# An mLSTM and HGRN2 decoder layer on one core: order of clearing, weight splits and the first head's convolution

## The chip, the core and the metric

The kernel runs on one core of a Trainium2 chip. The core has a matrix engine (TensorE, PE below; its weight loads are listed as PEld), and three engines that work on elements: VectorE (DVE), ScalarE (ACT) and GpSimd (POOL). SyncE (SP) issues the DMA transfers. Each engine runs its own instructions in order and waits for semaphores. PE writes to banks of PSUM; DVE and ACT read them from there, which is called an evacuation below. The metric is device time in microseconds, the median of several executions; lower is better.

## What is computed

One inference step of one layer, for 1024 prompt tokens and 8 sequences of 8 tokens (1088 tokens in all), in float32. The input is normalised and multiplied with one large matrix; its columns feed an mLSTM group of 4 heads and an HGRN2 group of 8 heads, whose results are multiplied with an output matrix. Cut to what the change touches:

```python
xn = rmsnorm(x, g_norm)
proj = xn @ w_in                     # 1024 x 7168
xm, zm, om, fh, qh, ih, zh = split(proj)
xc, conv_new = causal_conv(xm, conv_buf, conv_w, conv_b)   # 4 taps
xc = silu(xc)
q, k = per head: xc_h @ w_q, xc_h @ w_k
v = per head: xm_h @ w_v
gates = concat([q, k, v]) @ w_gate + b_gate
ig, lf = gates[..., :4], log_sigmoid(gates[..., 4:])
# mLSTM: running maximum m_t = max(logD over s <= t, cumsum(lf) + m0), then
#   decayed products of q, k and v by chunks
# HGRN2: S_t = diag(f_t) S_{t-1} + k_t v_t^T, o_t = S_t^T q_t, by levels of halving blocks
y = x + concat([hm, oh]) @ w_out
```

## The kernel before

**Split operands.** A float32 product is made from three matmuls of rounded operands: every operand is split into a high part (a cast on ACT) and a low part (a subtraction on DVE or POOL). Lines 94, 95 and 96 are the three matmuls. The normalised input lies in XH and XL.

**Blocks.** `w_in` is worked in blocks of 128 columns. `blk_load` loads a block's raw weights (wraw, three buffers, shared with the weights of q, k and v), `blk_split` splits them (line 147: whi on ACT, wlo on DVE for blocks in `v_splits`, else on POOL; two buffers each). `in_block` (line 246) multiplies a block with the tokens in three pieces of 384, 384 and 320 columns, each in one PSUM bank of a pool of three (`ps_mm`), and calls an evacuation for each piece. When it starts on a block it loads the block after next and splits the next one.

**The front.** Blocks 0 to 7 are xm, two for each of the 4 mLSTM heads. Blocks 0 and 1 run together while the input is still being normalised and transposed, then comes `front_v(0)` (v and the gates of head 0: nine tiles of 128 tokens, six matmuls each), block 2 (`third`), `front_qk(0)` (q and k: eight tiles of 272 columns, six matmuls each), block 3 (`fourth`). Head h of the next three then has `front_v(h)`, block 2h+2, `front_qk(h)` and block 2h+3.

- The evacuation of a piece of xm (`evac` in `front_conv`) makes mh (L477, ACT), a copy XB for the convolution (L478, ACT) and ml (L479, DVE); the last piece has copies for the 64 sample tokens besides (L481 and L482 on ACT, L483 on DVE). The bank is free when all of them have read it.
- `convolve` is a generator with one step at a time: four operations over 1112 columns on DVE (L503 once, L506 three times), a sigmoid on ACT (L514, L515), a product on DVE (L517, L518), the write of xc to memory, the split of xc (xch, L520 on ACT; xcl, L522, on DVE for the first head and on POOL for the others).
- `front_v` copies every tile out with two ACT copies, L540 (values) and L541 (gates, into GTOK for head 0 and GST for the others).

Up to block 3 the order on PE, ACT, DVE and POOL is that in which the code is written (`manual_schedule` in the main part, which calls `next` on the convolutions `c0`, `c1` of head 0 at hand-picked points). After it a scheduler orders all engines but keeps each engine's order fixed in the compiled program; behind the gates PE's order is by hand again. `behind(i, r)` adds an order on instruction i to come after r.

**The gates' scan.** `gate_scan` writes the gates to memory, reads them back as rows of tokens (lf, t1, ig, y), clears one column in t1 (L604), and runs two scans on DVE. It runs beside the first HGRN2 head (`hgrn_main(0)`), whose first level needs the products Q (L1022, L1023) and K (L987) from ACT and DVE; PE's first level is a burst of small matmuls at L101. `ctxs["k2"]` is set to a copy on DVE right behind K's.

Of the kernel before, what the change touches and what calls it, by code (L numbers as in the profile page):

```python
# [17 lines left out]
T = 1088  # L18
TP = 1024
# [11 lines left out]
def hybrid_step(  # L31
# [8 lines left out]
    V, S, G, PE = nc.vector, nc.scalar, nc.gpsimd, nc.tensor  # L40
# [78 lines left out]
    r = 0  # L119
# [22 lines left out]
    def w_split(key, eng=G):  # L142
        raw = wq[key]
        hi = wp.tile([P, 1024], F32R, tag="whi", name=nm("whi"))
        lo = wp.tile([P, 1024], F32R, tag="wlo", name=nm("wlo"))
        wq[key] = (hi.rearrange("p (k c) -> p k c", c=P), lo.rearrange("p (k c) -> p k c", c=P))
        return S.copy(hi, raw), eng.tensor_tensor(lo, raw, f32(hi), op=ALU.subtract)  # L147
# [16 lines left out]
    def blk_load(i):  # L164
        if i < len(blocks) and ("w", i) not in wq:
            kind, j = blocks[i]
            o = boff[kind] + j * P
            return w_load(("w", i), w_in[0, :, o:o + P].rearrange("(k p) c -> p k c", p=P))

    def blk_split(i, eng=None):  # L170
        if i < len(blocks) and not isinstance(wq[("w", i)], tuple):
            return w_split(("w", i), eng or (V if i in v_splits else G))
# [78 lines left out]
    def in_block(*items):  # L251


        ws = []
        for kind, j, evac in items:
            i = bidx[(kind, j)]
            if i > 1 or len(items) == 1:
                if ("w", i) in wq and not isinstance(wq[("w", i)], tuple):
                    blk_split(i)
            ws.append(i)  # L260
        for i in ws:
            blk_load(i + 2)
        nxt = ws[-1] + 1
        if len(items) == 1:
            blk_split(nxt)
        for c, (t0, n) in enumerate(CH):
            xh, xl = xchunk(XH, c), xchunk(XL, c)
            for (kind, j, evac), i in zip(items, ws):
                wh, wl = wq[("w", i)]
                ps = ps_mm()  # L270
                for k in range(8):
                    mm3(ps[:, :n], (wh[:, k, :], wl[:, k, :]), (xh[:, k, :], xl[:, k, :]), k == 0, k == 7)
                    if k % 2 and k < 7:
                        yield cost(6, n)
                evac(c, t0, n, ps)
                yield cost(6, n)
# [8 lines left out]
    ctxs = {}  # L285
# [93 lines left out]
    def behind(i, r):  # L379

        if r is None:
            return
        tc.add_manual_dep(getattr(i, "ins", i), getattr(r, "ins", r).name, mybir.DependencyInfo(
            mybir.DependencyClass.NoSync, mybir.DependencyReason.DATA), reason="behind")
# [42 lines left out]
    GTOK = cp.tile([P, 9, 8], F32, name="GTOK")  # L427
    GST = cp.tile([P, 9, 8], F32, name="GST")
# [96 lines left out]
    def front_v(h):  # L525
        wh, wl = qkv_w[h]
        xms = [fr[2 * h + a]["m"] for a in range(2)]
        for t in range(9):
            ps = ps_mm()
            u = t % 2  # L530
            if u == 0:
                vt = half("vt")
                vv = vt[:, :2 * VW].rearrange("p (a c) -> p a c", c=VW)
                G.memset(vv[:, :, 256:257], 1.0)
                G.memset(vv[:, :, 257:258], 0.0)
            for a in range(2):
                o = 512 + a * 264
                mm3(ps[:, :264], (xms[a][0][:, t * P:(t + 1) * P], xms[a][1][:, t * P:(t + 1) * P]),
                    (wh[:, o:o + 264], wl[:, o:o + 264]), a == 0, a == 1)
            S.copy(vv[:, u, 0:256], ps[:, :256])  # L540
            S.copy((GST if h else GTOK)[:, t, :], ps[:, 256:264])  # L541
            if t == 8:
                nc.sync.dma_start(out=vsd[h], in_=vt[:, :VW])
            elif u:
                nc.sync.dma_start(out=vd[h, :, (t - 1) * VW:(t + 1) * VW], in_=vt[:, :2 * VW])
            yield

        if h:
            V.tensor_tensor(GTOK, GTOK, GST, op=ALU.add)
# [33 lines left out]
    def gate_scan():  # L583

        ig, y, lf, t1, m, b = [unit(s)[0:4, :T] for s in ("ig", "gy", "glf", "gt", "gm", "gb")]

        lg = half("lg")
        LF = lg[:, 0:272]
        V.tensor_scalar(GT, GT, scalar1=bgt, scalar2=None, op0=ALU.add)
        S.activation(LF, GT, AF.Abs)  # L590
        S.activation(LF, LF, AF.Exp, scale=-1.0)
        S.activation(LF, LF, AF.Ln, bias=1.0)
        V.scalar_tensor_tensor(LF, GT, 0.0, LF, op0=ALU.min, op1=ALU.subtract)
        for i, src in enumerate((GT, LF)):
            nc.sync.dma_start(out=gd[i], in_=src)
        for i, dst in ((1, lf), (1, t1), (0, ig), (0, y)):
            nc.sync.dma_start(out=dst.rearrange("p (j t) -> p j t", t=272),
                              in_=gd[i].rearrange("(j r) t -> r j t", r=32)[4 * i:4 * i + 4])
        yield 1.0
        lfs = lf[:, TP:T].rearrange("p (b c) -> p b c", c=8)[:, :, 0]  # L600
        igs = ig[:, TP:T].rearrange("p (b c) -> p b c", c=8)[:, :, 0]
        lm = small(8, "lm")
        behind(V.tensor_tensor(lm[0:4, :], lfs, m0t, op=ALU.add), ctxs["k2"])
        V.memset(t1[:, TP:T].rearrange("p (b c) -> p b c", c=8)[:, :, 0], -1e30)  # L604
        V.tensor_tensor(y[:, TP:T].rearrange("p (b c) -> p b c", c=8)[:, :, 0], igs, lm[0:4, :], op=ALU.max)
        V.tensor_tensor_scan(m, t1, y, initial=0.0, op0=ALU.add, op1=ALU.max)
        yield 4.0
        G.memset(t1, 1.0)
        G.memset(t1[:, 0:TP].rearrange("p (b c) -> p b c", c=P)[:, :, 0], 0.0)
        G.memset(t1[:, TP:T].rearrange("p (b c) -> p b c", c=8)[:, :, 0], 0.0)  # L610
        st = lf[:, 0:TP].rearrange("p (b c) -> p b c", c=P)[:, 1:8, 0]
        V.tensor_tensor(st, st, m[:, 0:TP].rearrange("p (b c) -> p b c", c=P)[:, 0:7, 127], op=ALU.add)
        V.tensor_copy(lfs, lm[0:4, :])
        V.tensor_tensor_scan(b, t1, lf, initial=0.0, op0=ALU.mult, op1=ALU.add)
        V.tensor_tensor(y, b, m, op=ALU.subtract)
        nc.sync.dma_start(out=rd, in_=y)
        V.tensor_tensor(ig, ig, b, op=ALU.subtract)
        nc.sync.dma_start(out=o_pm[0, 0].unsqueeze(1), in_=m[:, TP - 1:TP])
        msl = small(8, "msl")
        V.tensor_copy(msl[0:4, :], m[:, TP:T].rearrange("p (b c) -> p b c", c=8)[:, :, 7])  # L620
        nc.sync.dma_start(out=o_sm[0].rearrange("b h -> h b"), in_=msl[0:4, :])
        yield 6.5
        ps = ps_o()
        for t in range(8):
            PE.transpose(ps[:, t * 8:t * 8 + 4], ig[:, t * P:t * P + P], ident[0:4, 0:4])
            PE.transpose(ps[:, t * 8 + 4:t * 8 + 8], m[:, t * P:t * P + P], ident[0:4, 0:4])
        for j in range(4):
            for o, src in ((64, ig), (68, m)):
                PE.matmul(ps[32 * j:32 * j + 32, o:o + 4], lhsT=src[:, TP + win(j):TP + win(j) + 32],
                          rhs=ident[0:4, 0:4], start=True, stop=True)  # L630
        V.tensor_copy(COLS.rearrange("p a b -> p (a b)"), ps[:, :72])
        S.activation(COLS[:, :, 4:8], COLS[:, :, 4:8], AF.Exp, scale=-2.0)
        yield 0.5

        co = unit("co")
        for kk in range(2):
            pt = ps_o()
            for k in range(4):
                PE.transpose(pt[:27, k * P:(k + 1) * P], CS[:, kk * 4 + k, :], ident)
            V.tensor_copy(co[:27, kk * 512:(kk + 1) * 512], pt[:27, :])  # L640
        nc.sync.dma_start(out=o_pconv[0, 0], in_=co[0:3, :DM])
        nc.sync.dma_start(out=o_sconv[0].rearrange("b j d -> (b j) d"), in_=co[3:27, :DM])
        yield 0.5
# [765 lines left out]
    def run(gen):  # L1409
        for _ in gen:  # L1410
            pass
# [56 lines left out]
    with tc.manual_schedule(engines={ET.PE, ET.Activation, ET.DVE, ET.Pool}):  # L1468
# [63 lines left out]
        blk_split(2, V)  # L1532
        run(prep)
        c0, c1 = convs
        next(c0)
        run(islice(first, 4))
        run(first)
        next(c0)
        next(c1)
        run(front_v(0))  # L1540
        next(c0)
        convs = []
        third = front_conv(1, (2,), convs)
        prep = qkv_prep(1)
        next(prep)
        run(islice(third, 2))
        next(c0)
        next(c1)
        run(islice(third, 2))
        next(c1)  # L1550
        run(c0)
        next(c1)
        run(islice(third, 4))
        run(c1)
        next(prep)
        run(islice(third, 4))
        run(third)
# [164 lines left out]
```

## Time and profile before

| | before |
|---|---|
| median of 3 runs | 1149.5 us (1148.18 to 1153.0) |
| profiled execution, its own time | 1149.5 us |
| its span, first to last instruction | 1147.7 us |
| mean granted TensorE clock | 0.995 |
| ACT busy | 471.1 us (41%) |
| POOL busy | 239.7 us (21%) |
| moved by DMA | 133.53 MB, mean 116 GB/s |

A row of the timeline has the start, the duration, the engine, the line, the operation, output and inputs by the program's names without their numbers, shape, and how many instructions were merged; in brackets stands how long the engine was idle before it, and what ended that. A row of the view of waits has engine, tile and line that waited, what it waited for, total, times and longest. A row of the view by windows has the stretch, its length, busy time of PE, PEld, DVE, ACT and POOL, the granted clock (1.00 is full), the DMA engines' share and GB/s.

### The profile page before, as it was taken

What the parts mean: (1) busy time and instruction counts of PE and PEld (TensorE: products, weight loads), DVE (VectorE), ACT (ScalarE), POOL (GpSimd) and SP (SyncE); (2) the same over time, 40 slices, a digit from 0 to 9 for tenths busy, and PEclk for the clock granted to TensorE, in tenths of its full rate; (3) what the DMA queues carried; (4) which work ended last, traced back from release to release, by engine and by line L of the source; (5) the groups of instructions that cost most, each with busy time, mean ns of one, the idle gap of its engine ahead of it and who ended that gap; (6) DMA issues with size and microseconds to landing.
All of it is one profiled execution on the core that took longest, in us unless ns stands there. A gap on an engine that the chain in (4) does not pass through costs nothing.

```text
span 1147.7 us, 22956 instructions
## 1 busy us (share of the span) xinstructions
PE 1123.9 (98%) x9255; PEld 1056.0 (92%) x9255; DVE 749.7 (65%) x1484; ACT 471.1 (41%) x1047; POOL 239.7 (21%) x396
## 2 busy tenths in 40 slices
PE   7989999899999999999999999999999999999997
PEld 6889999899999999999999999999999998888886
DVE  6656454494778567784779567877677687545533
ACT  6455455335432553235423453252524344243332
POOL 3204333002530144203530153102020200100000
PEclk9999999999999999999999999999999999999999
DMA  7243342222324242334124331422221255567662
GB/s 225 85 150 123 113 157 101 86 56 94 104 83 152 60 152 78 119 95 136 56 78 153 117 112 60 134 77 78 57 78 57 68 171 159 153 196 208 191 191 91
DMA packets 154154, 133.53 MB, mean 116 GB/s; under 512 B 11500, under 2 KB 130376, under 8 KB 154048
## 3 DMA queue, kind: packets, MB, share of 16 engines
q1 hardware_dynamic: 154046, 132.06, 36.9%
q8 instruction: 73, 1.20, 0.4%
q14 instruction: 33, 0.27, 0.1%
q10 hardware_dynamic: 2, 0.00, 0.0%
HBM read 93.47 MB, written 38.57 MB: 115 GB/s over the span
## 4 chain that ended last, share of the span: by engine, by line
PE 88%; DVE 5%; ACT 3%; DMA 2%; issue 2%; POOL 0%; SPq 0%; POOLq 0%; DVEq 0%; ACTq 0%
PE mm L94 24%; PE mm L95 23%; PE mm L96 23%; PE lv L101 2%; PE o L1216 1%; PE o L1235 1%; PE o L94 1%; PE o L95 1%; PE o L96 1%; PE o L1238 1%; DMA mraw<-mixd 1%; PE lv L1197 1%; PE o L1130 1%; PE mm L1338 1%; PE mm L1340 1%
## 5 line engine op out<-in xcount | busy, mean ns | idle before, releaser
L94 PE MATMUL mm<-XH,whi 128*128 128x384 f32 (+1 forms) x1344 | 450.4, 335 | 0.0
L95 PE MATMUL mm<-XL,whi 128*128 128x384 f32 (+1 forms) x1344 | 439.4, 327 | 0.4 <-DVE XL L245 0.4
L96 PE MATMUL mm<-XH,wlo 128*128 128x384 f32 (+1 forms) x1344 | 439.2, 327 | 0.0
L94 PEld LDWEIGHTS mm<-XH,whi 128*128 128x128 f32 x1344 | 253.5, 189 | 3.1 <-issue 2.5
L95 PEld LDWEIGHTS mm<-XL,whi 128*128 128x128 f32 x1344 | 253.5, 189 | 1.8 <-issue 0.9
L96 PEld LDWEIGHTS mm<-XH,wlo 128*128 128x128 f32 x1344 | 252.9, 188 | 0.0
L147 ACT CAST whi<-wraw 128x1024 fp32r<-128x1024 f32 x54 | 56.7, 1051 | 87.2 <-PE mm L95 67.2
L147 POOL TENSOR_TENSOR wlo<-wraw,whi 128x1024 fp32r<-128x1024 f32 x30 | 71.8, 2392 | 84.3 <-ACT whi L147 84.0
L1328 ACT CAST mhi<-mraw 128x1024 fp32r<-128x1024 f32 (+1 forms) x32 | 31.9, 998 | 69.3 <-PE mm L95 50.5
L974 POOL MEMSET A<- 128x288 f32 x8 | 2.7, 342 | 261.8 <-ACT A L1103 261.8
L94 PE MATMUL mm<-XH,mhi 128*128 128x512 f32 x144 | 56.8, 395 | 0.0
L96 PE MATMUL mm<-XH,mlo 128*128 128x512 f32 x144 | 56.3, 391 | 0.2 <-DVE mlo L1329 0.2
L95 PE MATMUL mm<-XL,mhi 128*128 128x512 f32 x144 | 56.1, 389 | 0.0
L1329 DVE TENSOR_TENSOR mlo<-mraw,mhi 128x1024 fp32r<-128x1024 f32 (+1 forms) x32 | 37.0, 1155 | 20.2 <-ACT mhi L1328 19.7
L922 DVE TENSOR_SCALAR f<-f,OML,LB 128x384 f32<-128x384 f32 (+1 forms) x24 | 32.9, 1369 | 10.7 <-ACT f L920 10.3
L479 DVE TENSOR_TENSOR xml<-mm,xmh 128x384 fp32r<-128x384 f32 (+1 forms) x24 | 12.3, 511 | 42.2 <-ACT XB L478 42.2
L96 PE MATMUL mm<-woh,mlo 128*128 128x512 f32 x96 | 37.5, 390 | 0.0
L147 DVE TENSOR_TENSOR wlo<-wraw,whi 128x1024 fp32r<-128x1024 f32 x24 | 29.3, 1220 | 12.5 <-ACT whi L147 12.5
L94 PE MATMUL mm<-woh,mhi 128*128 128x512 f32 x96 | 37.4, 389 | 0.0
L95 PE MATMUL mm<-wol,mhi 128*128 128x512 f32 x96 | 37.4, 389 | 0.0
L990 DVE TENSOR_TENSOR QK<-hk,Sf 128x256 f32<-128x256 f32 x96 | 36.1, 416 | 0.0
L1401 POOL TENSOR_TENSOR rs<-rs,mhalf 128x1 f32<-128x1 f32 (+1 forms) x9 | 4.9, 542 | 145.9 <-DVE rs L1400 145.9
(365 smaller groups left out, 2201.0 us busy)
## 6 DMA issues: line engine op xcount, KB each, us to landing
wraw<-in_w_in SPq DMA_DIRECT2D x56, 512.0 KB
woraw<-in_w_out SPq DMA_DIRECT2D x16, 512.0 KB
mraw<-mixd SPq DMA_DIRECT2D x16, 512.0 KB
mraw<-mixd SPq DMA_DIRECT2D x16, 448.0 KB
xcd<-XB SPq DMA_DIRECT2D x8, 544.0 KB
qkd<-qk SPq DMA_DIRECT2D x16, 272.0 KB
xcr<-xcd SPq DMA_DIRECT2D x8, 544.0 KB
mixd<-xcr SPq DMA_DIRECT2D x8, 544.0 KB
```

Source lines behind the costliest of these rows:

```text
L94: PE.matmul(out, lhsT=lh, rhs=rh, start=first, stop=False)
L95: PE.matmul(out, lhsT=lh, rhs=rl, start=False, stop=False)
L96: PE.matmul(out, lhsT=ll, rhs=rh, start=False, stop=last)
L101: i = PE.matmul(out, lhsT=lhsT, rhs=rhs, start=start, stop=stop)
L147: return S.copy(hi, raw), eng.tensor_tensor(lo, raw, f32(hi), op=ALU.subtract)
L479: evs.append(V.tensor_tensor(ml[:, t0:t0 + m], ps[:, :m], f32(mh[:, t0:t0 + m]), op=ALU.subtract))
L922: V.tensor_scalar(f[:, s], f[:, s], scalar1=OML[:, h:h + 1], scalar2=LB[:, h:h + 1], op0=ALU.mult, op1=ALU.add)
L990: i = V.tensor_tensor(dst, ksrc, ssrc, op=ALU.mult)
L1130: PE.transpose(pt[:, u * P:(u + 1) * P], iT[:, t * P:(t + 1) * P], ident)
L1197: PE.transpose(tp[:, u * P:(u + 1) * P], sq[:, u * P:(u + 1) * P], ident)
L1328: S.copy(hi[:, :w * n], raw[:, :w * n])
L1329: V.tensor_tensor(lo[:, :w * n], raw[:, :w * n], f32(hi[:, :w * n]), op=ALU.subtract)
```

## The change

Three things are put elsewhere in the order; no operation is added or removed.

1. In `gate_scan` the clearing of one column of t1 comes behind `ctxs["k2"]`.
2. `in_block` no longer splits block 3 when block 2 starts; the main part does so, on DVE, behind the first head's convolutions. For later blocks, where a `front_v` ran ahead, the cast of the next block's weights comes behind the gates' copy of v's second tile.
3. The steps of the first head's convolutions: those that stood ahead of the second block's last evacuation come behind it, all steps over the 1112 columns follow each other, and the remaining steps of both come in one run within block 2.

```diff
@@ in_block
-        if len(items) == 1:
-            blk_split(nxt)
+        if len(items) == 1 and nxt > 3:
+            r = blk_split(nxt)
+            if "v1" in ctxs:
+                behind(r[0], ctxs.pop("v1"))
@@ front_v
-            S.copy((GST if h else GTOK)[:, t, :], ps[:, 256:264])
+            gc = S.copy((GST if h else GTOK)[:, t, :], ps[:, 256:264])
+            if t == 1:
+                ctxs["v1"] = gc
@@ gate_scan
-        V.memset(t1[:, TP:T].rearrange("p (b c) -> p b c", c=8)[:, :, 0], -1e30)
+        behind(V.memset(t1[:, TP:T].rearrange("p (b c) -> p b c", c=8)[:, :, 0], -1e30), ctxs["k2"])
@@ the main part
         c0, c1 = convs
-        next(c0)
         run(islice(first, 4))
         run(first)
         next(c0)
+        next(c0)
+        next(c1)
         next(c1)
         run(front_v(0))
         next(c0)
+        next(c1)
+        next(c0)
+        next(c1)
         convs = []
         third = front_conv(1, (2,), convs)
         prep = qkv_prep(1)
         next(prep)
         run(islice(third, 2))
-        next(c0)
-        next(c1)
+        run(c0)
         run(islice(third, 2))
-        next(c1)
-        run(c0)
-        next(c1)
+        run(c1)
+        blk_split(3, V)
         run(islice(third, 4))
-        run(c1)
         next(prep)
```

In the rows below names have the program's numbers; lines of the changed kernel are 2 to 5 higher than before.

DVE at the end of the second block, before: XB_250 and XB_254 are the two convolutions' inputs, Y their sums, mm_564 the bank of the second block's last piece, wraw_260 the raw weights of block 3, mm_722 the third block's first piece.

```order
L503 TENSOR_SCALAR Y_561<-XB_250,PAR 128x1112
L506 SCALAR_TENSOR_TENSOR Y_561<-XB_250,PAR,Y_561 128x1112
L479 TENSOR_TENSOR xml_257<-mm_564,xmh_256 128x256
L483 TENSOR_TENSOR xml_257<-mm_564,xmh_256 128x128
L506 SCALAR_TENSOR_TENSOR Y_561<-XB_250,PAR,Y_561 128x1112 x2
L503 TENSOR_SCALAR Y_600<-XB_254,PAR 128x1112
L506 SCALAR_TENSOR_TENSOR Y_600<-XB_254,PAR,Y_600 128x1112
L147 TENSOR_TENSOR wlo_719<-wraw_260,whi_718 128x1024
L517 TENSOR_TENSOR XB_250<-Y_561,XB_250 128x1024
L518 TENSOR_TENSOR XB_250<-Y_561,XB_250 128x64
L506 SCALAR_TENSOR_TENSOR Y_600<-XB_254,PAR,Y_600 128x1112 x2
L479 TENSOR_TENSOR xml_715<-mm_722,xmh_714 128x384
```

The same place of the changed kernel, from the second half of the evacuation on (mm_559 is the second block's last piece, its first half stands just ahead); mm_732 is the third block's first piece.

```order
L485 TENSOR_TENSOR xml_257<-mm_559,xmh_256 128x128
L505 TENSOR_SCALAR Y_593<-XB_250,PAR 128x1112
L508 SCALAR_TENSOR_TENSOR Y_593<-XB_250,PAR,Y_593 128x1112 x3
L505 TENSOR_SCALAR Y_600<-XB_254,PAR 128x1112
L508 SCALAR_TENSOR_TENSOR Y_600<-XB_254,PAR,Y_600 128x1112 x3
L519 TENSOR_TENSOR XB_250<-Y_593,XB_250 128x1024
L520 TENSOR_TENSOR XB_250<-Y_593,XB_250 128x64
L519 TENSOR_TENSOR XB_254<-Y_600,XB_254 128x1024
L520 TENSOR_TENSOR XB_254<-Y_600,XB_254 128x64
L524 TENSOR_TENSOR xcl_707<-XB_250,xch_706 128x1088
L481 TENSOR_TENSOR xml_729<-mm_732,xmh_728 128x384
L524 TENSOR_TENSOR xcl_711<-XB_254,xch_710 128x1088
```

Both convolutions now run through behind the evacuation, and the split of block 3 has gone behind the second xcl: it is the row after the last one shown, followed by the evacuation of the third block's second piece.

ACT at the start of `front_v(1)`, before: mm_1012 is the last piece of block 3, mm_1066, mm_1078 and mm_1088 are v's first three tiles, wraw_937 the raw weights of block 5.

```order
L147 CAST whi_1184<-wraw_937 128x1024
L477 CAST xmh_935<-mm_1012 128x256
L478 COPY XB_933<-mm_1012 128x256
L540 COPY vt_1067<-mm_1066 128x256
L541 COPY GST<-mm_1066 128x8
L540 COPY vt_1067<-mm_1078 128x256
L541 COPY GST<-mm_1078 128x8
L481 COPY XB_933<-mm_1012 128x8x8
L482 CAST xmh_935<-mm_1012 128x128
L540 COPY vt_1089<-mm_1088 128x256
```

And in the changed kernel:

```order
L479 CAST xmh_935<-mm_1012 128x256
L480 COPY XB_933<-mm_1012 128x256
L542 COPY vt_1067<-mm_1066 128x256
L543 COPY GST<-mm_1066 128x8
L483 COPY XB_933<-mm_1012 128x8x8
L484 CAST xmh_935<-mm_1012 128x128
L542 COPY vt_1067<-mm_1078 128x256
L543 COPY GST<-mm_1078 128x8
L147 CAST whi_1184<-wraw_937 128x1024
L542 COPY vt_1089<-mm_1088 128x256
```

The cast of block 5 has moved from ahead of the evacuation to behind the second tile's copies, and the last evacuation's second half (L483, L484) ahead of the second tile's; heads 2 and 3 have the same. On POOL the subtraction of the same split moves behind two small copies (L500, L501). On SP the load that waits for that split moves behind two more writes of v.

DVE at the first level, before: hq is the HGRN2 query, wlo_2378 the low part of a later block's weights, Q_319 and K_320 are what the level multiplies, glf and gt are the gates' rows lf and t1.

```order
L604 MEMSET gt_2342 4x8
L147 TENSOR_TENSOR wlo_2378<-wraw_2252,whi_2377 128x1024
L930 TENSOR_TENSOR hq_2062<-hq_2062,mm_2312 128x320
L1023 TENSOR_TENSOR Q_319_2364<-hq_2062,f_2060 128x544
L987 COPY K_320_2367<-hk_2061 128x256
L987 COPY K_320_2367<-hk_2061 128x4x64
L1038 COPY Sf_2363<-f_2060 128x544
L603 TENSOR_TENSOR lm_2459<-glf_2341,m0t 4x8
```

And in the changed kernel:

```order
L147 TENSOR_TENSOR wlo_2378<-wraw_2252,whi_2377 128x1024
L934 TENSOR_TENSOR hq_2062<-hq_2062,mm_2312 128x320
L1027 TENSOR_TENSOR Q_319_2364<-hq_2062,f_2060 128x544
L991 COPY K_320_2367<-hk_2061 128x256
L991 COPY K_320_2367<-hk_2061 128x4x64
L1042 COPY Sf_2363<-f_2060 128x544
L607 TENSOR_TENSOR lm_2459<-glf_2341,m0t 4x8
L608 MEMSET gt_2342 4x8
```

The clearing has moved behind K's copies and Sf's, and behind the sum that already waited for them.

## Prediction

> **What bounds the kernel now.** Line numbers are those of the kernel before; times are µs from the start of the span. The page first:
>
> ```profile
> span 1147.7 us, 22956 instructions
> PE 1123.9 (98%) x9255; PEld 1056.0 (92%) x9255; DVE 749.7 (65%) x1484; ACT 471.1 (41%) x1047; POOL 239.7 (21%) x396
> ```
>
> TensorE (PE) is busy 98% of the span. The change adds no arithmetic and, by the compiled order, leaves PE's own order as it was. So it can only act on the moments in which PE stands still, or runs slowly. The view of waits, for PE alone, names them (total, times, longest); three of its rows lie where the diff lies:
>
> ```profile
> PE lv L101 <- DVE K L987: 2.9, 1, 2.9
> PE mm L95 <- DVE xcl L522: 2.2, 1, 2.2
> PE mm L94 <- ACT GST L541: 1.3, 3, 0.4
> ```
>
> I then read the timeline, engine by engine, around each. The profiled execution took 1149.5, its span plus 1.8, and that is also the median of the three runs, so a saving in this trace is subtracted from 1149.5 as it stands.
>
> **Term A: the bank of the second block's last piece.**
>
> ```profile
> 54.16 0.39 PE L94 MATMUL mm<-wqh,xmh 128*128 128x264 f32 x1 [1.61 <-ACT GTOK L541]
> ...
> 51.01 0.38 ACT L478 COPY XB<-mm 128x256 f32<-128x256 f32 x1
> ...
> 51.64 1.38 DVE L506 SCALAR_TENSOR_TENSOR Y<-XB,PAR,Y 128x1112 f32<-128x1112 f32 x1
> 52.94 0.41 DVE L479 TENSOR_TENSOR xml<-mm,xmh 128x256 fp32r<-128x256 f32 x1
> 53.80 0.29 DVE L483 TENSOR_TENSOR xml<-mm,xmh 128x128 fp32r<-128x128 f32 x1 [0.45 <-ACT xmh L482]
> ```
>
> ACT's copy ends at 51.39, but DVE takes a convolution step first and begins the evacuation L479 at 52.94; ACT's last copies wait behind L479, v's copies behind those, and PE's third v tile until 54.16. With the convolution behind the evacuation, L479 starts at 51.42 and the pair L479 to L483 takes 54.09 − 52.94 = 1.15, so the bank is free at 52.58 and PE starts at 52.65. **A = 1.5.** Best and worst: 1.6, the whole wait, and 0.
>
> **Term B: the first q and k tiles.**
>
> ```profile
> 71.58 0.38 PE L94 MATMUL mm<-xch,wqh 128*128 128x272 f32 x1
> ...
> 75.37 0.60 PE L95 MATMUL mm<-xcl,wqh 128*128 128x272 f32 x1 [2.15 <-DVE xcl L522]
> ...
> 79.01 0.29 PE L94 MATMUL mm<-xch,wqh 128*128 128x272 f32 x1
> ...
> 82.87 1.20 PE L101 MATMUL o<-qk,front 128*32 128x272 f32 x16
> ```
> ```profile
> 54.16:56.00 1.84, 1.84 (x15) 1.84 (x16) 1.80 (x2) 0.81 (x5) 1.28 (x3) 1.00 0.38 140
> 75.40:78.60 3.20, 3.02 (x12) 2.73 (x13) 2.34 (x5) 1.08 (x4) 0.28 (x3) 0.50 0.21 64
> ```
>
> Eight tiles of six matmuls run from 71.58 to 82.87: 11.29. The last five, from 79.01, take 3.86, so 0.77 each, and eight at that pace would take 6.2. The other 5.1 are waits and, by the second row of the second fence (granted clock, third number from the end), 3.2 µs at half clock right behind the longest of them. When are the operands there in the changed order?
>
> ```profile
> 54.00 2.78 DVE L506 SCALAR_TENSOR_TENSOR Y<-XB,PAR,Y 128x1112 f32<-128x1112 f32 x2
> 56.70 0.86 DVE L503 TENSOR_SCALAR Y<-XB,PAR 128x1112 f32<-128x1112 f32 x1
> ...
> 63.51 1.23 DVE L147 TENSOR_TENSOR wlo<-wraw,whi 128x1024 fp32r<-128x1024 f32 x1 [4.54 <-ACT whi L147]
> 64.65 1.22 DVE L517 TENSOR_TENSOR XB<-Y,XB 128x1024 f32<-128x1024 f32 x1
> ...
> 65.92 2.78 DVE L506 SCALAR_TENSOR_TENSOR Y<-XB,PAR,Y 128x1112 f32<-128x1112 f32 x2
> ...
> 68.62 0.55 DVE L479 TENSOR_TENSOR xml<-mm,xmh 128x384 fp32r<-128x384 f32 x1
> ...
> 74.03 1.28 DVE L522 TENSOR_TENSOR xcl<-XB,xch 128x1088 fp32r<-128x1088 f32 x1
> ...
> 77.30 0.29 DVE L483 TENSOR_TENSOR xml<-mm,xmh 128x128 fp32r<-128x128 f32 x1 [0.45 <-ACT xmh L482]
> ```
> ```profile
> 66.03 1.10 ACT L520 CAST xch<-XB 128x1088 fp32r<-128x1088 f32 x1 [2.56 <-DVE XB L518]
> ...
> 67.41 0.49 ACT L478 COPY XB<-mm 128x384 f32<-128x384 f32 x1
> ```
>
> From 52.5 DVE runs both convolutions through: each one L503 (0.88 to the next start) and three L506 (2.70 for two, so 1.35 each), 4.93; two end at 62.4. The 4.5 that DVE sat idle before 63.51, held by the split of block 3 that itself waited behind v's copies on ACT, go. Two products L517 with L518 (64.65 to 65.92: 1.27 each) end at 64.95. ACT casts the second xch to 66.1 and takes the third block's first piece to 66.9 (both ACT rows together: 1.87 from 66.03); DVE answers with xml (0.55) and then the second xcl (1.28): ready at 68.7. PE, 1.5 earlier by A, asks for it from 70.1 on: 1.4 of cover, and the waits of B are gone.
>
> **What is late next:** the third tile needs the bank of the third block's last piece, which L483 frees. Before, that came 77.59 − 74.03 = 3.56 after the second xcl began. Now the split of block 3 (1.14 to the next start) and one more xml (0.55) stand between: 67.4 + 3.56 + 1.69 = 72.6. PE has done two tiles at 70.07 + 1.55 = 71.6, so it waits **a new 1.1** until 72.7; six tiles (4.63) later the gate part starts at 77.3 instead of 82.9. Less A, **B = 4.0**. With no new wait it would be 5.1. With one of 2.15 it would be 3.0, and with the half clock back, which costs half of 3.2, 1.4. The first row of the second fence, behind A's wait of 1.6, has full clock, so I take full clock.
>
> The Trainium skill, "TensorE: Matmul & The Clock Gate", Part 1, has the clock halved after an idle window of about 3.4 µs, on windows that run freely. By it neither wait here (2.15, and 2.93 in D) would have to cost any clock, and the gain would be 3.0 less (a rival below); the row shows the half clock behind a wait of 2.15, so the sum goes by the row.
>
> Block 3's split itself is used only by the fourth block, behind the gate part. On SP the load of block 5's raw weights now waits for it, behind two xc writes; block 5's cast stands at 97.31 in a row of C, over 20 µs of cover. POOL's small history copies only change places.
>
> **Term C: three heads' v tiles.** One head stands for three (the wait row says three times 0.4):
>
> ```profile
> 97.25 0.28 PE L94 MATMUL mm<-wqh,xmh 128*128 128x264 f32 x1
> ...
> 103.97 0.28 PE L94 MATMUL mm<-wqh,xmh 128*128 128x264 f32 x1
> ...
> 104.70 0.34 PE L94 MATMUL mm<-XH,whi 128*128 128x384 f32 x1
> ```
> ```profile
> 97.31 1.05 ACT L147 CAST whi<-wraw 128x1024 fp32r<-128x1024 f32 x1 [0.97 <-PE mm L95]
> ...
> 100.36 0.37 ACT L540 COPY vt<-mm 128x256 f32<-128x256 f32 x1 [0.49 <-ACT xmh L482]
> ```
> ```profile
> 98.43 2.39 POOL L147 TENSOR_TENSOR wlo<-wraw,whi 128x1024 fp32r<-128x1024 f32 x1
> ```
> ```profile
> 99.81 1.61 DVE L503 TENSOR_SCALAR Y<-XB,PAR 128x1112 f32<-128x1112 f32 x1 [0.46 <-ACT XB L481]
> ```
>
> Nine tiles take 7.45; the last alone takes 0.73, nine of them 6.57. So 0.88 is lost, not only the 0.4 that the wait names. The cast of the next block stands on ACT ahead of the last evacuation and of v's first copies. Moved behind the second tile's copies, it lets them start 0.9 earlier, and the third tile finds its bank. The fifth tile now takes the bank that L483 frees: L503 starts about 98.9, takes 0.86 (row 56.70) instead of 1.61, because POOL's subtraction no longer runs until 100.82, and L483 ends near 100.0; PE asks at 97.25 + 4 × 0.73 = 100.2. The cast sits between 99.3 and 100.4; the third tile's two copies end by 101.0 at most, and the sixth tile asks at 100.9. Margins of 0.1 to 0.2, so I take the full 0.88: **C = 2.6** for three. Queued behind the cast are seven tiles' copies; if each tile waited out the whole cast, C would be 2.6 − 3 × 1.05 = −0.5.
>
> **Term D: the clearing ahead of the first level.**
>
> ```profile
> 222.25 0.07 DVE L604 MEMSET gt<- 4x8 f32 x1 [5.05 <-DMA gt<-gd]
> 222.33 1.22 DVE L147 TENSOR_TENSOR wlo<-wraw,whi 128x1024 fp32r<-128x1024 f32 x1
> ```
> ```profile
> 218.03 1.05 ACT L147 CAST whi<-wraw 128x1024 fp32r<-128x1024 f32 x1 [1.43 <-PE mm L95]
> ```
> ```profile
> 225.26 0.90 PE L101 MATMUL lv<-Q,K 128*32 128x64 f32 x32 [2.93 <-DVE K L987]
> ...
> 229.04 0.33 PE L95 MATMUL mm<-XL,whi 128*128 128x384 f32 x1
> ```
> ```profile
> 356.62 0.65 PE L101 MATMUL lv<-Q,K 128*32 128x64 f32 x32
> ...
> 358.96 0.33 PE L95 MATMUL mm<-XL,whi 128*128 128x384 f32 x1
> ```
>
> A clearing of 4 by 8 elements holds DVE's queue 5.05 until a transfer lands. PE starts the first level 2.93 after the split at 222.33. Without the clearing the split runs when its cast ends, 219.1, and the level is ready at 222.05; PE is free at 222.33. So the wait of 2.93 goes. From there to the eighth matmul behind the level took 3.78, the same stretch in the next such stage 2.34: 1.44 of slow clock go too. **D = 4.4.** The clearing now stands where DVE arrives at about 222.2, as the transfer lands, so it waits for little; behind it are scans that PE reads much later. Lower end 0, if the copies into K are held by the same transfer.
>
> **Sum:** 1.5 + 4.0 + 2.6 + 4.4 = 12.5; 1149.5 − 12.5 = **1137.0**, 1.1% less.
>
> **Rivals.**
> - *The new wait in B grows past 2 µs and brings the half clock back.* For it: the chain to 72.5 has no gap on DVE. Against: it needs another 1.05. Then B = 1.4: **1139.6**. Chance 0.14.
> - *D does not come*, the change not doing there what it says. For it: K's copies wait on a transfer too. Against: nothing shows one of theirs in flight at 221. **1141.4**. Chance 0.08.
> - *The slow clock is not tied to these waits* (the page's window). The waits go but the slow rows stay, 1.6 in B and 1.4 in D: **1140.0**. Chance 0.04.
> - *Given back later.* Row 222.25 shows that a transfer can hold a queue for 5 µs; a load later on that is set by something other than PE would be met earlier, and PE would wait. Against: loads here are issued when buffers come free, which moves with PE. Half back or more: **1144 to 1149**. Chance 0.09.
> - *Slower.* The cast among v's copies, three times, makes PE wait as long as in D: each place then costs 2.93 + 1.44 and its 0.88 is not won, 5.25 × 3 = 15.8 against 12.5: **1152.8**. It turns the sign from a wait of about 1.9 each; the cast is 1.05 long and has 0.1 of margin. Chance 0.05.
>
> **The numbers.** The forecast has 0.60, with 1134 to 1140 of its own. To hold 8 in 10 the range takes in the next three: 1133.5 (no new wait in B, and a run 1.3 under the median as the lowest of the three was) to 1143.0. A measurement tells about 0.5% from no change: faster by more has 0.87, the same 0.11, slower 0.02.
>
> **What would show it.** In the changed profile, PE's waits should no longer name L987, the xcl or GTOK rows; one new wait near 1 µs should stand at the third q tile; the clock should be 1.00 around 70 to 78 and 217 to 224; v's nine tiles of the later heads should take 6.6. A wait of over 2 µs in any of these places, or a new one after 230, would make the prediction wrong.

## The result and the profile after

| | before | after |
|---|---|---|
| median of 4 runs each, µs | 1149.38 | 1136.86 |
| lowest to highest | 1148.18 to 1153.0 | 1135.51 to 1138.68 |
| ratio, 95% interval | | 0.9887 [0.9864, 0.9909] |
| profiled execution (span) | 1149.5 (1147.7) | 1136.34 (1134.6) |

The kernel is 12.5 µs faster; 12.5 was forecast. Lines of the changed kernel stand 2 to 5 higher than those of before (L479 is now L481, L483 L485, L503 L505, L506 L508, L522 L524, L541 L543, L604 L608, L987 L991). First the page's busy times and then PE's four largest waits, both of the kernel after:

```profile
span 1134.6 us, 22961 instructions
PE 1117.3 (98%) x9255; PEld 1051.3 (93%) x9255; DVE 753.9 (66%) x1484; ACT 471.4 (42%) x1047; POOL 240.7 (21%) x396
```
```profile
PE lv L239 <- DVE xsq L222: 4.2, 4, 2.3
PE o L1477 <- DMA g<-in_g_norm: 2.5, 1, 2.5
PE mm L94 <- DVE xml L485: 1.2, 2, 1.0
PE mm L95 <- DVE XL L245: 0.6, 1, 0.6
```

The three rows of before that lay where the diff lies (K, xcl, GST), and the GTOK row, are gone. One row has grown: xml, from 0.2 to 1.2 in two pieces. PE has the same 9255 matmuls, and its busy time fell by 6.6, from 1123.9 to 1117.3. Part of that are matmuls that count as busy for longer, of which there are fewer: the one of 75.37 in the prediction's rows, at half clock, took 0.60, and the one of 71.64 below, which starts behind a wait, 0.37, where 0.28 or 0.29 is usual.

Where the 13.1 µs between the two spans came from is read by lining up PE's matmuls, which stand in the same order in both, and noting how far the kernel after is ahead:

| place on PE | start before | start after | ahead by | gained there |
|---|---|---|---|---|
| first head's third v tile (end of A) | 54.16 | 51.52 | 2.64 | 1.25 in the start-up, 1.4 in A |
| first q tile | 71.58 | 68.89 | 2.69 | |
| gate part (end of B) | 82.87 | 76.31 | 6.56 | 3.87 in B |
| behind the v tiles of heads 1 to 3 (C) | 182.98 | 173.99 | 8.99 | 2.43 in C |
| eighth matmul behind the first level (D) | 229.04 | 215.62 | 13.42 | 4.43 in D |
| end of the span | 1147.7 | 1134.6 | 13.1 | −0.3 |

The start-up's 1.25 lies ahead of 21 µs, before anything that the change touches; it is a difference between two executions, of which more below. Most of it comes from a few matmuls that follow each other every 0.32 in the kernel before and every 0.17 in the one after. One of them, first of before and then of after:

```profile
17.34 0.52 PE L96 MATMUL mm<-XH,wlo 128*128 128x384 f32 x1
```
```profile
16.84 0.34 PE L96 MATMUL mm<-XH,wlo 128*128 128x384 f32 x1
```

The view's granted clock is 1.00 at both places, so it doesn't show why. Without the start-up the change gained 12.1 in A to D and gave back 0.3.

The rows of the kernel after that answer to those of the prediction, PE's timeline at A, B, C and D in turn (start, duration, instruction, and in brackets the wait ahead of it):

```profile
51.52 0.36 PE L94 MATMUL mm<-wqh,xmh 128*128 128x264 f32 x1 [0.18 <-DVE xml L485]
...
68.89 0.38 PE L94 MATMUL mm<-xch,wqh 128*128 128x272 f32 x1
...
71.64 0.37 PE L94 MATMUL mm<-xch,wqh 128*128 128x272 f32 x1 [0.99 <-DVE xml L485]
...
76.31 1.20 PE L101 MATMUL o<-qk,front 128*32 128x272 f32 x16
...
90.70 0.28 PE L94 MATMUL mm<-wqh,xmh 128*128 128x264 f32 x1
...
97.33 0.34 PE L94 MATMUL mm<-XH,whi 128*128 128x384 f32 x1
...
213.28 0.65 PE L101 MATMUL lv<-Q,K 128*32 128x64 f32 x32
...
215.62 0.33 PE L95 MATMUL mm<-XL,whi 128*128 128x384 f32 x1
```

In B the eight tiles take 76.31 − 68.89 = 7.42 instead of 11.29; in C nine v tiles take 97.33 − 90.70 = 6.63 instead of 7.45; in D the level starts without a wait, and 2.34 instead of 3.78 pass to the eighth matmul. VectorE in B and D, kernel after:

```profile
66.33 1.28 DVE L524 TENSOR_TENSOR xcl<-XB,xch 128x1088 fp32r<-128x1088 f32 x1
67.53 1.22 DVE L147 TENSOR_TENSOR wlo<-wraw,whi 128x1024 fp32r<-128x1024 f32 x1
...
71.20 0.29 DVE L485 TENSOR_TENSOR xml<-mm,xmh 128x128 fp32r<-128x128 f32 x1 [0.45 <-ACT xmh L484]
...
210.17 1.23 DVE L147 TENSOR_TENSOR wlo<-wraw,whi 128x1024 fp32r<-128x1024 f32 x1 [1.97 <-ACT whi L147]
...
213.34 0.07 DVE L608 MEMSET gt<- 4x8 f32 x1
```

The second low half is there at 67.61, and PE asks for it at 69.49. Block 3's split stands between it and L485, which frees the bank of the third q tile at 71.49; PE starts it at 71.64. The clearing L608 waits for nothing where it stands now.

### The profile page after: what moved, and what is told of

It is laid out like the page before. It is cut to its first block, busy times and chain, and to the rows that moved or that the text cites. A ratio compares the mean times of both kernels' runs of the same rounds, so it can differ in the third digit from the quotient of the medians.

```text
span 1134.6 us, 22961 instructions
## 1 busy us (share of the span) xinstructions
PE 1117.3 (98%) x9255; PEld 1051.3 (93%) x9255; DVE 753.9 (66%) x1484; ACT 471.4 (42%) x1047; POOL 240.7 (21%) x396
## 4 chain that ended last, share of the span: by engine, by line
PE 90%; DVE 4%; DMA 3%; ACT 1%; issue 1%; POOL 0%; SPq 0%; POOLq 0%; ACTq 0%; DVEq 0%
PE mm L94 25%; PE mm L96 24%; PE mm L95 24%; PE lv L101 2%; PE o L1220 1%; DMA mraw<-mixd 1%; PE o L1239 1%; PE o L94 1%; PE o L95 1%; PE o L96 1%; PE o L1242 1%; PE lv L1201 1%; PE o L1134 1%; PE lv L746 1%; PE lv L768 1%
## 5 line engine op out<-in xcount | busy, mean ns | idle before, releaser
L508 DVE SCALAR_TENSOR_TENSOR Y<-XB,PAR,Y 128x1112 f32<-128x1112 f32 x24 | 39.0, 1626 | 0.5
L481 DVE TENSOR_TENSOR xml<-mm,xmh 128x384 fp32r<-128x384 f32 (+1 forms) x24 | 12.3, 512 | 36.6 <-ACT XB L480 36.6
```

What stands on the lines that cost most here:

```text
L481: evs.append(V.tensor_tensor(ml[:, t0:t0 + m], ps[:, :m], f32(mh[:, t0:t0 + m]), op=ALU.subtract))
L508: V.scalar_tensor_tensor(Y[:, :1112], XB[:, j:j + 1112], cw[:, 8 * j + ft:8 * j + ft + 1], Y[:, :1112], op0=ALU.mult, op1=ALU.add)
```

## The experiments

**The three parts, each alone on the kernel before.** The clearing alone:

```diff
-        V.memset(t1[:, TP:T].rearrange("p (b c) -> p b c", c=8)[:, :, 0], -1e30)
+        behind(V.memset(t1[:, TP:T].rearrange("p (b c) -> p b c", c=8)[:, :, 0], -1e30), ctxs["k2"])
```

> The kernel before with the clearing alone moved (term D). My theory: the wait of 2.93 ahead of the first level goes, and with it 1.44 of slow clock, 4.4 in all: about 1145.1 against 1149.4; the profile shows no wait at the level and granted clock 1.00 behind it. Rival 1, K's copies wait for something else: 1149.4 and a wait of about 2.9 under another name. Rival 2, the slow clock is not tied to the wait: 2.9 less, 1146.5, with a half-clock stretch near the level.

Measured: 1144.84 against 1150.02, ratio 0.9962 [0.9946, 0.9977], so 4.4 µs. PE's timeline, at a stage that was not touched otherwise:

```profile
222.24 0.65 PE L101 MATMUL lv<-Q,K 128*32 128x64 f32 x32
```

No wait stands ahead of the level, and to the eighth matmul behind it 2.34 pass. K's copies wait for no transfer of their own: rival 1 falls. D is as it was worked out.

The casts alone:

```diff
-            blk_split(nxt)
+            r = blk_split(nxt)
+            if nxt > 3 and "v1" in ctxs:
+                behind(r[0], ctxs.pop("v1"))
...
-            S.copy((GST if h else GTOK)[:, t, :], ps[:, 256:264])
+            gc = S.copy((GST if h else GTOK)[:, t, :], ps[:, 256:264])
+            if t == 1:
+                ctxs["v1"] = gc
```

> The kernel before with only the casts of heads 1 to 3 moved behind the second v tile's copies (term C). My theory: nine v tiles take 6.6 instead of 7.45 in each of three heads, 2.5 in all: about 1146.9, and the row GST <- 1.3 leaves PE's waits. Rival 1, only the wait that the trace names goes: 1.3, so 1148.1. Rival 2, the cast stalls PE between v's tiles: slower, up to 1152.

Measured: 1147.11, ratio 0.997 [0.9956, 0.9984], so 3.4 (1.8 to 5.1). The first and the last row here are the start of head 1's v tiles and of what follows them:

```profile
98.47 0.28 PE L94 MATMUL mm<-wqh,xmh 128*128 128x264 f32 x1
...
105.11 0.34 PE L94 MATMUL mm<-XH,whi 128*128 128x384 f32 x1
```

6.64 for the nine tiles, as after the whole change, and GST is gone from the waits. That is 0.81 less than the 7.45 of before, near the 0.88 that the prediction took and not the 0.4 that the wait names. Lined up, 0.6 to 0.7 of it stands at the third tile, which had waited, and the rest within the tiles behind it.

The first head's order alone (on the kernel before: no split for block 3 at the start of its block, and the order of the main program as in the diff's last part):

```diff
-        if len(items) == 1:
+        if len(items) == 1 and nxt > 3:
             blk_split(nxt)
```

> The kernel before with only the first head's order (both convolutions behind the second block's last evacuation, block 3's split behind them; terms A and B). My theory: 1.4 + 3.9 = 5.3 less, about 1144.1, with one new wait of about 1.0 at the third q tile and clock 1.00 there. Rival, the gain of B hangs on the other parts of the change (the three parts do not add): under 4 less, over 1145.4.

Measured: 1143.57, ratio 0.9942 [0.9921, 0.9963], so 6.7 (4.3 to 9.1). From the first q tile to the gate part it took 7.41, with one wait of 0.98. The three parts give 4.4, 3.4 and 6.7, together 14.5 against 13.0 (10.5 to 15.6) for the whole change: they add, within their intervals.

**Which half of the first head's order makes B?** Two kernels take it apart. In the first, the changed kernel has block 3's split back where it was; in the second, the kernel before has only that split moved.

```diff
-        if len(items) == 1 and nxt > 3:
+        if len(items) == 1:
             r = blk_split(nxt)
-            if "v1" in ctxs:
+            if nxt > 3 and "v1" in ctxs:
...
-        blk_split(3, V)
```

> The changed kernel with block 3's split put back to the start of the third block, the convolutions' new order kept. In this order the split stands on VectorE behind both convolutions' products and ahead of both low halves, on ScalarE behind v's copies. My theory: it is the convolutions' place that gave B; the split's 1.14 stands ahead of the same evacuation in either place, so the first q tile to the gate part takes 7.0 to 7.8 as now: 1136.4 to 1137.3. Rival, VectorE's 4.54 behind the split was the cause of B: the wait for the second low half comes back, 2 us or more, with the half clock: 1139 to 1141.

Measured: 1137.99, ratio 0.9897 [0.988, 0.9914]. VectorE and PE of this kernel:

```profile
65.50 1.23 DVE L147 TENSOR_TENSOR wlo<-wraw,whi 128x1024 fp32r<-128x1024 f32 x1 [2.12 <-ACT whi L147]
```
```profile
69.64 0.39 PE L95 MATMUL mm<-xcl,wqh 128*128 128x272 f32 x1 [0.44 <-DVE xcl L524]
...
72.47 0.37 PE L94 MATMUL mm<-xch,wqh 128*128 128x272 f32 x1 [1.34 <-DVE xml L485]
```

The stretch took 8.71 (68.44 to 77.15): 1.3 more than after, where I expected 0.4 more at most. The split held VectorE again, but only for 2.12, because both convolutions were already through. The waits were 0.44 and 1.34, none reached 2, and the granted clock is 1.00 from 69 to 77. So in these traces the order of the convolutions alone takes 11.29 to 8.71, and the split's place the rest; by the clock of the whole kernel, 1137.99 and 1136.86 are too near each other to tell.

```diff
-        if len(items) == 1:
+        if len(items) == 1 and nxt > 3:
...
         run(c1)
+        blk_split(3, V)
         next(prep)
```

> The kernel before with only block 3's split moved behind the second convolution (its place among the others kept). My theory: the hold of 4.54 goes and the second low half is ready by about 72.4, so the waits of 0.61 and 2.15 go; but the split then stands ahead of the third block's last evacuation, which frees the third q tile's bank near 75.8, asked for at 73.1: a wait of 2.7 in their place, with half clock behind it. 0 to 2 less: 1147.4 to 1149.4. Rival, the split alone is B: 4 less, 1145.4.

Measured: 1149.61 against 1149.81, ratio 0.9993 [0.998, 1.0007]: no change. PE, and the clock (third number from the end) in the 6 µs behind the longer wait:

```profile
73.21 0.39 PE L95 MATMUL mm<-xcl,wqh 128*128 128x272 f32 x1 [0.83 <-DVE xcl L522]
76.71 0.56 PE L94 MATMUL mm<-xch,wqh 128*128 128x272 f32 x1 [2.23 <-DVE xml L483]
83.93 1.20 PE L101 MATMUL o<-qk,front 128*32 128x272 f32 x16
```
```profile
76.71:82.71 6.00, 6.00 (x27) 6.00 (x28) 0.45 (x1) 1.50 (x5) 0.00 (x0) 0.53 0.68 216
```

The waits of 0.61, 2.15 and 0.18 (2.94) became 0.83 and 2.23 (3.06). VectorE at two places of this kernel:

```profile
62.47 1.23 DVE L517 TENSOR_TENSOR XB<-Y,XB 128x1024 f32<-128x1024 f32 x1 [3.44 <-ACT XB L514]
...
76.28 0.29 DVE L483 TENSOR_TENSOR xml<-mm,xmh 128x128 fp32r<-128x128 f32 x1 [0.45 <-ACT xmh L482]
```

Of VectorE's idle 4.54 most stayed: without the split, the product L517 stands next and waits 3.44 for ScalarE's sigmoid L514. It starts 2.18 earlier than before (64.65), but the split, 1.14, now stands ahead of the last evacuation, so L483 comes only 1.02 earlier (77.30 before) and the wait moves from the low half to the bank. The third q tile starts 1.02 earlier too, at 76.71 instead of 77.73; the half clock behind the new wait then lasts longer, and the stretch takes 12.31 instead of 11.29. What this move is worth without the slow clock, the runs' times don't tell.

**How near is C to turning?** The changed kernel with the cast one tile earlier:

```diff
-            if t == 1:
+            if t == 0:
                 ctxs["v1"] = gc
```

> The changed kernel with the cast one tile earlier, behind the first v tile's copies, for heads 1 to 3. My theory: it then stands ahead of the evacuation's last two copies and the second tile's, whose banks are asked for with 0.1 to 0.2 of margin; 1.05 later, they make PE wait about 0.8 in each head, so all of C is given back: 1139.3. Rival, there is slack of a tile: no change, 1136.9.

Measured: 1143.66, ratio 0.9947 [0.9933, 0.9962]: 6.8 over the changed kernel, more than twice what I expected. PE, then VectorE and GpSimd at head 1:

```profile
94.53 0.39 PE L94 MATMUL mm<-wqh,xmh 128*128 128x264 f32 x1 [0.57 <-ACT GST L543]
...
97.17 0.39 PE L94 MATMUL mm<-wqh,xmh 128*128 128x264 f32 x1 [0.92 <-DVE xml L485]
```
```profile
94.08 2.83 DVE L505 TENSOR_SCALAR Y<-XB,PAR 128x1112 f32<-128x1112 f32 x1 [1.24 <-ACT XB L483]
96.84 0.28 DVE L485 TENSOR_TENSOR xml<-mm,xmh 128x128 fp32r<-128x128 f32 x1
```
```profile
93.94 2.38 POOL L147 TENSOR_TENSOR wlo<-wraw,whi 128x1024 fp32r<-128x1024 f32 x1 [1.19 <-ACT whi L147]
```

The place was right, the price was not. The convolution step L505 now begins 0.14 behind GpSimd's subtraction and takes 2.83. In the changed kernel it starts ahead of that subtraction and takes 0.86:

```profile
92.36 0.86 DVE L505 TENSOR_SCALAR Y<-XB,PAR 128x1112 f32<-128x1112 f32 x1 [0.36 <-ACT XB L483]
```

PE waits twice in each head, where the changed kernel doesn't: 0.57 for ScalarE's copies, near the 0.8 that was expected, and 0.92 more for L485, which stands behind the convolution step. Each head loses 1.9 against the changed kernel in the lined-up matmuls (1.93, 1.90 and 2.01), 5.8 in all. The two spans differ by 7.6; 0.9 of the rest lies in the start-up, and the other 0.9 was not traced. Both waits are under 1 µs, and the granted clock from 94.53 to 100.53 is 1.00.

**The new wait in B.** The changed kernel with the split one place later:

```diff
-        blk_split(3, V)
         run(islice(third, 4))
         next(prep)
         run(islice(third, 4))
         run(third)
+        blk_split(3, V)
```

> The changed kernel with block 3's split moved once more, behind the third block's last evacuation. My theory: the new wait of 0.99 at the third q tile hangs on the 1.14 that the split takes on VectorE ahead of that evacuation, so it goes to 0.1 or less: about 1135.9 against 1136.9, front from the first q tile to the gate part 6.4 instead of 7.42. Rival 1, the evacuation waits for ScalarE (0.45 are named there) or for the two subtractions of the next head's weights, and the wait stays at 0.5 or more. Rival 2, the split now delays the transposed weights' copy that PE needs, and the time comes back within the next 10 us: 1136.9.

Measured: 1136.78, ratio 0.9882 [0.9864, 0.9899], which a measurement cannot tell from the changed kernel's 0.9887. In the trace the wait is gone: from the first q tile (71.35) to the gate part (77.96) it takes 6.61 instead of 7.42, a gain of 0.81, of which 0.16 is given back at the next block. Theory and trace agree on the wait; the 0.65 µs that is left of 1137 is too small for these runs to confirm.

**Does a wait bring the half clock?** Products put ahead of K's copies make the first level late by a chosen time (two, three, four of them; they write a buffer that is overwritten next):

```diff
         K1 = unit("K1")
+        if h == 0:
+            for _ in range(2):
+                behind(V.tensor_tensor(K1[:, 0:544], f[:, 0:544], f[:, 0:544], op=ALU.mult), q1)
```

> The changed kernel with 2 products of 128 by 544 (0.67 each, into a buffer that is overwritten next) put ahead of K's copies at the first level: PE waits about 1.35 there. My theory (half clock follows a wait over 2 us, not one of 1.6): clock 1.00 behind it, the level to the eighth matmul behind it 2.34, cost 1.35. Rival by the Trainium skill's page TensorE: Matmul & The Clock Gate, Part 1 (an idle window of about 3.4 us): the same here. Rival, any wait over 1 us brings it: cost 2.8.

> The same with 3 products: a wait of about 2.0. My theory: half clock for about 3.2 us behind it, level to eighth matmul 3.8. Rival by the page's window: clock 1.00, 2.34.

> The same with 4 products: a wait of about 2.7. My theory: half clock for about 3.2 us, level to eighth matmul 3.8. Rival by the page's window: clock 1.00, 2.34, which would leave the slow clock of the kernel before at this place to something other than its wait of 2.93.

The level's row of each, in this order, from PE's timelines:

```profile
216.56 0.65 PE L101 MATMUL lv<-Q,K 128*32 128x64 f32 x32 [1.61 <-DVE K L991]
```
```profile
218.73 1.08 PE L101 MATMUL lv<-Q,K 128*32 128x64 f32 x32 [5.70 <-DVE K L991]
```
```profile
221.81 1.08 PE L101 MATMUL lv<-Q,K 128*32 128x64 f32 x32 [6.48 <-DVE K L991]
```

Two products did nearly what they should: a wait of 1.61 (1.35 was expected) and full clock, 1.00 in the 6 µs behind it. The one run took 1141.25, 4.4 over the changed kernel's median; lined up, 1.6 of that lies in the start-up and 1.7 at the level. Three and four missed their aim: with them the scan of 2.40 and the next level's products were ordered ahead of K's copies on VectorE, and the waits became 5.70 and 6.48, with a granted clock of 0.59 and 0.52 in the 6 µs behind them (1143.56 and 1147.24, one run each). So they say nothing on waits of 2 to 3 µs.

The other runs do. At the level the kernel with only the first head's order had waited 2.54 and showed full clock behind it; casts_alone waited 2.55 and had a granted clock of 0.72 over the 6 µs from its level's start. I ran the former twice more:

> The same kernel as first_head_alone once more, for the clock behind its wait of 2.54 at the first level; that run showed full clock there, while casts_alone had 3.9 of half clock behind a wait of 2.55. My first theory (a wait over 2 us brings half clock) fails in one of the two already. Theory now: a window that runs freely decides, so the same wait brings half clock in some executions and not in others, and the level to the eighth matmul behind it takes 2.3 in some and up to 3.8 in others. Rival: the other parts of the program decide, and this kernel shows 2.3 each time.

> The same again, on the same terms: 2.3 behind the level if the program decides, 2.3 to 3.8 if the phase of a free window does; the start-up before 25 us likewise with 0 to 1.5 of slow clock that differs from run to run.

The level's row and the granted clock in the 6 µs from its start, for the three executions of this one kernel (first_head_alone, then the two repeats):

```profile
218.98 0.65 PE L101 MATMUL lv<-Q,K 128*32 128x64 f32 x32 [2.54 <-DVE K L987]
```
```profile
218.98:224.98 6.00, 6.00 (x110) 5.97 (x111) 6.00 (x14) 1.09 (x7) 2.13 (x6) 1.00 0.25 75
```
```profile
219.89 1.08 PE L101 MATMUL lv<-Q,K 128*32 128x64 f32 x32 [2.72 <-DVE K L987]
```
```profile
219.89:225.89 6.00, 6.00 (x94) 5.96 (x95) 6.00 (x15) 0.57 (x4) 2.13 (x6) 0.50 0.24 69
```
```profile
219.28 1.08 PE L101 MATMUL lv<-Q,K 128*32 128x64 f32 x32 [2.50 <-DVE K L987]
```
```profile
219.28:225.28 6.00, 6.00 (x101) 5.96 (x102) 6.00 (x15) 0.56 (x4) 2.13 (x6) 0.72 0.27 79
```

Clock 1.00, 0.50 and 0.72 behind waits of 2.54, 2.72 and 2.50: from the level's start to the 24th matmul behind it 5.09, 7.76 and 6.49 passed. The rival, that the program decides, falls: one program, three outcomes. The wait of 2.15 in B shows the same: 3.2 µs of half clock behind it in the kernel before, and about 7 in casts_alone, where the granted clock from 75.10 to 82.10 is 0.52 and B's stretch takes 12.80 (71.30 to 84.10) instead of 11.29.

The times of the three executions follow in the same order: 1141.87, 1145.8 and 1143.72; up to 0.6 of the differences lies in the start-up.

## Why the prediction was right, and where it was not

The forecast's 12.5 is also the difference of the medians, and that it fits to the tenth is luck: the traces give 12.1 for the four terms, 0.3 given back and 1.25 of start-up that no term holds, and the interval of the ratio reaches from 10.5 to 15.6. The mechanisms of the four terms are what the runs bear out.

- **Term A** (1.5): 1.4. PE's wait of 1.61 is 0.18, and L481 with L485 stands ahead of the convolution as the order said.
- **Term B** (4.0): 3.87. The two waits and the half clock went. The step "what is late next" was right too: the third q tile waits for the third block's last evacuation, 0.99 where 1.1 was worked out, and split3_late shows that it hangs on the split's 1.14. What the prediction left open was which edit earns it: split3_back and split3_alone show that the convolutions' order must come first, and that the split's move is worth 1.3 with it in the traces and no measurable time without it.
- **Term C** (2.6): 2.43. The full 0.88 per head was the better choice over the named 0.4: 0.81 was measured. The margins were as small as stated, but the turning point was mis-priced: one tile earlier costs 1.9 per head, since a convolution step of 0.86 becomes one of 2.83 beside GpSimd. By the rival's price (5.25 per head) it would have been too dear, by my own expectation of 0.8 too cheap.
- **Term D** (4.4): 4.43 in the trace, 4.4 by the clearing alone.
- **Given back**: 0.3 against none in the forecast; the rival with half or more did not come.
- **The clock, the step that failed.** The prediction took full clock behind a wait of 1.6 and half clock behind one of 2.15 as a rule with a fixed price: 1.6 lost in B, 1.4 in D. The first half held in every mid-program trace that was read (waits of 0.99, 1.34 and 1.61: none). The second did not: 0 to 2.7 µs were lost at the level behind waits of 2.50 to 2.72. So the 1.6 in B and the 1.4 in D are one draw each (about 3.4 was another in B; 0, 1.4 and 2.7 at the level), and the sum met the median partly for that reason. Nor did the 2.15 in B stand alone: the wait of 0.61 had ended only 0.40 before the 2.15 began. The rival that left the slow clock in place was wrong as well: with the waits gone the granted clock is 1.00 in the stretches of A to D. The Trainium skill, "TensorE: Matmul & The Clock Gate", Part 1, says that the window runs freely and that the slow time at a kernel's start therefore varies from run to run; the three executions show the same in mid-program. By the Trainium skill the idle window is about 3.4 µs, longer than the waits of 2.15 to 2.93 that were enough here, and there the measurement decides. Why a wait shorter than the window can be enough wasn't tried.
- **The start-up**, 1.25 of the 13.1 between the two profiled spans, belongs to no term. It did not enter the forecast, which subtracts from the time before, and the medians differ by 12.5.

## What to carry to other kernels

Where one engine is busy 98% of the span, read the few places where it stands still, and for each follow the queue of the engine that releases it: an instruction that waits for a transfer or a cast there (a clearing of 0.07, a split of 1.2) holds everything behind it. When you take a hold out of a queue, work out what arrives last next; taking the split out of VectorE's idle stretch of 4.5 µs left 3.4 of it, now spent waiting for a sigmoid, and gained no measurable time, while with the convolutions' new order around it the stretch behind gained 3.9. Count a slow clock behind a wait of over 2 µs as a lottery over executions, not as a fixed price, and take its size from several profiles.

## What the runs showed of the hardware

- The slow clock behind a wait of 2.5 to 2.7 µs varied between none and 2.7 µs of lost time in one and the same program; behind waits of 0.99, 1.34 and 1.61 in mid-program the granted clock was 1.00 in every trace that was read there.
- VectorE's convolution step of 128 by 1112 (a tensor_scalar) took 0.86 when it began ahead of GpSimd's subtraction of 2.38, and 2.83 when that had begun 0.14 ahead of it. It ended 0.59 behind the subtraction, and the step of 1.61 in the prediction's rows, which began later within one, 0.60 behind (101.42 and 100.82). So the order of the two, by tenths of a microsecond, is worth 2 µs. The other way round, in clear_alone the step began 0.36 ahead of a subtraction (84.54) and took 0.85, and the subtraction took 2.75.
- In the first 25 µs, ahead of anything changed, two executions can differ by over 1 µs: 1.25 between the kernels before and after, and 2.5 between the changed kernel and split3_late, which is more than the gain of 0.65 there. In both pairs the slower one has matmuls of 0.52 there where the other has 0.34.
